# Four pairs of FFN gate blocks as two-by-two block products, seven in place of eight

## The chip, the cores and the metric

One core of a Trainium2 chip runs the whole program. The metric is the device time of one execution in microseconds; three runs of the kernel before gave 1250.42 to 1250.91, median 1250.7. Five engines work side by side, each on its own queue in order: TensorE (PE) multiplies, VectorE (DVE) and ScalarE (ACT) do elementwise work, GpSimd (POOL) does little here, and SyncE (SP) issues the loads.

## The reference

Two layers of a decoder trunk, all in float32, on 256 tokens of width 1024. Each layer is a norm, a wide input projection, three token mixers with gates, an output projection and then the feed-forward part. What the change touches is only this:

```
h = rmsnorm(x, norm_ffn[l])                     # 256 x 1024
x = x + (silu(h @ w_ffn_gate[l]) * (h @ w_ffn_up[l])) @ w_ffn_down[l]   # 1024 x 2816, 2816 x 1024
```

## The kernel before

Tokens lie as two tiles of 128 (t = 0, 1). A weight matrix is cut into blocks of 512 output columns, and the 1024 input features of a block into units of four rows of 128: a unit is one load of 1 MB (`load`, L982) into one of three raw buffers (`wr`). For accuracy each operand is split in a high part, rounded to the matmul's format ("hi", a cast on ScalarE, `conv_hi`, L1004), and the rest ("lo", a subtraction on VectorE of two SBUF inputs, `conv_lo`, L1010). A half unit (two rows of 128 by 512 columns, 1024 elements a partition) is converted at a time, into four rotating pairs of tiles (`wh`, `wl`). `products` (L1035) then issues, for each 128-row slice and each t, three matmuls of 512 columns: hi x hi, hi x lo, lo x hi (L1059 to L1061), so 24 per unit and 48 per block, into two PSUM banks of the pool `acc` (four banks). Four more banks (`sc`) serve the mixers and the transposes.

The order is written out by hand, in Python, at build time. The list `units` holds the units in order; in the FFN it is gate block 0 and up block 0 interleaved unit by unit, then gate b, up b for b = 1 to 4, then one block of the last 256 gate and 256 up columns, then the two down blocks. While a unit is multiplied there are four slots, one after every six matmuls; at each, `pump` runs the small steps that are due (`defer(n, ...)`: n slots later; `push`: a list of steps, one a slot), and one hi or one lo of a later unit is issued. `flush(key)` runs pumps until nothing with that key is left, so it puts all of it ahead of what comes next on every queue. At the start of unit i the load of unit i + 3 is issued.

A gate block is evicted by a tanh on ScalarE (L900) and a combine on VectorE (L904); an up block by a multiply on VectorE (L910), and its result is transposed on TensorE in two groups of four (`T_pair`, L297), each of which goes back to SBUF by a hi on ScalarE (L302) and a lo on VectorE (L309). Working tiles of 4 KB a partition come from the pool `s4` (19 tiles).

## Time and profile before

| | before |
|---|---|
| runs, median (lowest to highest) | 1250.7 us (1250.42 to 1250.91) |
| profiled execution, its own time | 1250.75 us |
| its span | 1248.9 us |
| busy TensorE / VectorE / ScalarE / GpSimd | 1238.5 / 786.4 / 659.6 / 34.8 us |
| mean granted TensorE clock | 0.999 |
| loads | 217 MB, 1 MB each, 5.0 us from issue to landing |

Busy time is the sum of the instructions' times on an engine; an instruction that waits inside for something the profile does not show counts as busy. The span runs from the first to the last instruction. All times of rows are microseconds from the span's start, means are in ns.

### The profile page before, as it was taken

Reading aid. Unit: us, or ns where it says so; the run is one execution under the profiler, and the core shown is the slowest. Engines: PE = TensorE matmul, PEld = TensorE weight load, DVE = VectorE, ACT = ScalarE, POOL = GpSimd, SP = SyncE. Lnnn points to the kernel's source line nnn. Section 1 sums busy time; section 2 is a strip of 40 time slices with the busy share of each in tenths; the row PEclk is TensorE's granted clock in tenths of the full one; section 3 lists DMA queues with packets and bytes.
Section 4 is the critical chain, followed back from the end, with each engine's and each line's share of the span. In section 5 each row is a group of like instructions: output and inputs, shape, how many; then the busy total and the mean of one; then the engine's idle time right before and its main releaser. Section 6 shows DMA issues by size and latency. Waiting matters only on the chain.

```text
span 1248.9 us, 17348 instructions
## 1 busy us (share of the span) xinstructions
PE 1238.5 (99%) x6894; PEld 1080.8 (87%) x6894; DVE 786.4 (63%) x1248; ACT 659.6 (53%) x999; POOL 34.8 (3%) x43
## 2 busy tenths in 40 slices
PE   9999999999999999999999999999999999999997
PEld 7999899999888888888889989898988888888886
DVE  5555567768566676565555565687775767656644
ACT  6433566766545455444454345667745445544442
POOL 1000000100000000000000000000000100000000
PEclk9999999999999999999999999999999999999999
DMA  8666445544655555555555543445456455555561
GB/s 280 213 207 196 154 167 169 163 144 168 201 169 169 170 189 181 186 184 185 185 184 187 189 156 129 148 157 169 136 203 199 138 168 182 189 188 182 178 219 59
DMA packets 114145, 219.82 MB, mean 176 GB/s; under 512 B 4168, under 2 KB 11336, under 8 KB 114064
## 3 DMA queue, kind: packets, MB, share of 16 engines
q1 hardware_dynamic: 113104, 217.07, 53.2%
q0 software_dynamic: 384, 0.84, 0.3%
q8 instruction: 54, 0.88, 0.3%
q10 hardware_dynamic: 576, 0.81, 0.2%
q14 instruction: 27, 0.22, 0.1%
HBM read 217.16 MB, written 1.54 MB: 175 GB/s over the span
## 4 chain that ended last, share of the span: by engine, by line
PE 98%; DMA 0%; issue 0%; DVE 0%; ACT 0%; POOLq 0%; POOL 0%; SPq 0%; DVEq 0%
PE acc L1060 22%; PE acc L1061 22%; PE acc L1059 22%; PE acc L1075 7%; PE acc L1074 7%; PE acc L1073 7%; PE tp L297 2%; PE sc L383 1%; PE sc L487 1%; PE sc L618 1%; PE sc L617 1%; PE sc L382 0%; PE sc L488 0%; PE tp L653 0%; PE acc L1025 0%; DMA x<-in_x_dram 0%
## 5 line engine op out<-in xcount | busy, mean ns | idle before, releaser
L1010 DVE TENSOR_TENSOR wl<-wr,wh 128x1024 fp32r<-128x1024 f32 x402 | 490.5, 1224 | 319.5 <-ACT wh L1004 317.0
L1004 ACT CAST wh<-wr 128x1024 fp32r<-128x1024 f32 x402 | 421.2, 1050 | 404.2 <-PE acc L1061 273.6
L1059 PE MATMUL acc<-wh,s 128*128 128x512 f32 x1220 | 488.8, 401 | 0.0
L1060 PE MATMUL acc<-wl,s 128*128 128x512 f32 x1220 | 476.0, 390 | 0.5 <-DVE wl L1108 0.5
L1061 PE MATMUL acc<-wh,s 128*128 128x512 f32 x1220 | 476.4, 390 | 0.0
L1061 PEld LDWEIGHTS acc<-wh,s 128*128 128x128 f32 x1220 | 229.3, 188 | 49.1
L1060 PEld LDWEIGHTS acc<-wl,s 128*128 128x128 f32 x1220 | 229.8, 188 | 45.0 <-DVE wl L1108 1.4
L1059 PEld LDWEIGHTS acc<-wh,s 128*128 128x128 f32 x1220 | 229.6, 188 | 44.2 <-issue 0.6
L1073 PE MATMUL acc<-s,wh 128*128 128x256 f32 x768 | 222.8, 290 | 0.0
L1075 PE MATMUL acc<-s,wl 128*128 128x256 f32 x768 | 217.4, 283 | 0.0
L1074 PE MATMUL acc<-s,wh 128*128 128x256 f32 x768 | 217.1, 283 | 0.0
L1074 PEld LDWEIGHTS acc<-s,wh 128*128 128x128 f32 x768 | 147.1, 192 | 0.3
L1073 PEld LDWEIGHTS acc<-s,wh 128*128 128x128 f32 x768 | 147.1, 191 | 0.3
L1075 PEld LDWEIGHTS acc<-s,wl 128*128 128x128 f32 x768 | 146.9, 191 | 0.0
L629 ACT ACTIVATE e<-e,sm 128x128 f32<-128x128 f32 x64 | 28.6, 448 | 9.8 <-DVE sm L622 9.6
L302 ACT CAST s<-tp 128x512 fp32r<-128x512 f32 x30 | 17.6, 587 | 27.2 <-PE tp L297 27.2
L305 ACT ACTIVATE s<-tp,gT 128x256 fp32r<-128x256 f32 x44 | 18.4, 472 | 18.7 <-PE tp L297 18.2
L297 PE MATMUL tp<-ident,s 128*128 128x128 f32 x184 | 27.5, 272 | 0.0
L297 PEld LDWEIGHTS tp<-ident,s 128*128 128x128 f32 x184 | 22.7, 140 | 5.2
L309 DVE TENSOR_TENSOR s<-tp,s 128x512 fp32r<-128x512 f32 x30 | 20.8, 692 | 10.1 <-ACT s L302 7.5
L312 DVE SCALAR_TENSOR_TENSOR s<-tp,gT,s 128x256 fp32r<-128x256 f32 x44 | 19.1, 478 | 12.4 <-ACT s L305 12.4
L622 DVE CUSTOM_DVE_ANT_0 e<-sc,bias_t 128x128 f32<-128x128 f32 x32 | 9.3, 289 | 24.6 <-PE sc L618 24.6
(173 smaller groups left out, 830.1 us busy)
## 6 DMA issues: line engine op xcount, KB each, us to landing
wr<-in_w_in_dram SPq DMA_DIRECT2D x107, 1024.0 KB, 5.1
wr<-in_w_ffn_gate_dram SPq DMA_DIRECT2D x20, 1024.0 KB, 5.0
wr<-in_w_ffn_up_dram SPq DMA_DIRECT2D x20, 1024.0 KB, 5.0
wr<-in_w_ffn_down_dram SPq DMA_DIRECT2D x20, 1024.0 KB, 5.1
wr<-in_w_branch_diff_dram SPq DMA_DIRECT2D x8, 1024.0 KB, 5.0
wr<-in_w_branch_ret_dram SPq DMA_DIRECT2D x8, 1024.0 KB, 5.0
wr<-in_w_out_dram SPq DMA_DIRECT2D x8, 1024.0 KB, 5.0
wr<-in_w_branch_dil_dram SPq DMA_DIRECT2D x4, 1024.0 KB, 5.1
```

Of the source, the lines that this page charges most:

```text
L297: T.transpose(pt[:, (2 * j + t) * P:(2 * j + t + 1) * P], srcs[t][:, j * P:(j + 1) * P], ident)
L309: V.tensor_tensor(lo[:, c0:c0 + 2, :], ptv, hi[:, c0:c0 + 2, :].bitcast(F32), op=ALU.subtract)
L312: V.scalar_tensor_tensor(lo[:, c0 + j, :], ptv[:, j, :], scale[j], hi[:, c0 + j, :].bitcast(F32), op0=ALU.mult, op1=ALU.subtract)
L629: A.activation(e[:, c], e[:, c], AF.Exp, bias=s_[:, 2 * m + qb:2 * m + qb + 1], scale=-1.0, accum_out=s_[:, 4 + 2 * m + qb:5 + 2 * m + qb])
L1004: A.copy(h, grans[i][0][:, ks, :])
L1010: V.tensor_tensor(l, grans[i][0][:, ks, :], pr[0].bitcast(F32), op=ALU.subtract)
L1059: T.matmul(o, sh, h[:, k, :], start=first, stop=False)
L1060: T.matmul(o, sh, l[:, k, :], start=False, stop=False)
L1061: T.matmul(o, sl, h[:, k, :], start=False, stop=last)
L1073: T.matmul(o, h[:, k, fs], xh[:, kk, :], start=first, stop=False)
L1074: T.matmul(o, h[:, k, fs], xl[:, kk, :], start=False, stop=False)
L1075: T.matmul(o, l[:, k, fs], xh[:, kk, :], start=False, stop=last)
```

## The change

Gate blocks 1 and 2 are taken as one block of 1024 columns, and so are 3 and 4, in both layers: four such pairs. For each 256 input features, the tokens form a two-by-two matrix of 128 x 128 blocks (token half by feature half) and the weights a two-by-two matrix of 128 x 512 blocks. In place of eight block products, seven products of sums are accumulated, each over four units, in seven PSUM banks (`Block7`, `products7`), each with the three matmuls of the split. A unit now holds 256 rows by 1024 columns, 1 MB as before.

The sums of weights are made on GpSimd (`sums7`: a subtraction of 1024 elements and two of 512 per unit) into two `s4` tiles; they are issued two units ahead. They are then converted like weights: seven blocks of 512 columns a unit, as parts of two, one, two and two blocks. The sums of tokens are made once per layer and feature group on GpSimd (`sums`), cast on ScalarE and subtracted on VectorE. After the last unit the seven accumulators are added up to the two gate blocks by seven additions on VectorE and a copy on ScalarE (`gate7`).

The conversions of all units go through one routine, `feed`, which issues the next hi or lo if fewer than four tile pairs are in use. The order of blocks is now: the pair of gates, then its two up blocks. The first unit of a pair flushes the evictions and the key "sums", the first up block behind it flushes "ffn". The second group of transposes of an up block is deferred by three slots more in place of two.

```diff
@@ -86,6 +86,22 @@
         self.accs = None
+class Block7:
+    nat = True
+    ORDER = ((1, 0, 0), (2, 0, 1), (3, 1, 0), (5, 2, 0), (7, 2, 1), (6, 3, 0), (4, 3, 1))
+    def __init__(self, w, npairs, tokens, steps, needs=None):
+        self.w, self.nks, self.tokens, self.steps = w, [2] * npairs, tokens, steps
+        self.needs = needs or {}
+        self.acc = {}
 @with_exitstack
 def trunk(ctx, tc, x_in, w_in, w_branch_ret, w_branch_diff, w_branch_dil, w_out, diff_lambda, rel_bias,
           w_ffn_gate, w_ffn_up, w_ffn_down, norm_final, gains, onehot, bmask, rot, decay, out):
@@ -890,7 +906,7 @@
         def ffn_h(z, w, dst):
             for c in range(w // S):
-                defer(2 + 2 * c, lambda c=c: T_pair([z[t][:, c * S:(c + 1) * S] for t in range(2)], dst, 2 * c, None),
+                defer(2 + 3 * c, lambda c=c: T_pair([z[t][:, c * S:(c + 1) * S] for t in range(2)], dst, 2 * c, None),
                       "ffn")
         def ffn_gate(zg, w):
@@ -910,13 +926,63 @@
                 V.scalar_tensor_tensor(z[t][:, :w], z[t][:, :w], st["nrm"].rsq[t], zu[t], op0=ALU.mult, op1=ALU.mult)
             ffn_h(z, w, dst)
+        L["z"] = []
         def ev_ffn_gate(accs):
-            L["z"] = ffn_gate(accs, 512)
+            L["z"].append(ffn_gate(accs, 512))
         def ev_ffn_up(accs):
             dst = new_T()
             L["hT"].append(dst)
-            ffn_up(L["z"], accs, 512, dst)
+            ffn_up(L["z"].pop(0), accs, 512, dst)
+        def sums(j):
+            nb, c = j // 2, 2 * (j % 2)
+            if c == 0:
+                L["sm", nb] = (S4([P, 2, 4, P], F32R), S4([P, 2, 4, P], F32R))
+            hi, lo = L["kf"][nb]
+            shi, slo = (t[:, j % 2] for t in L["sm", nb])
+            tmp = S4([P, 2, 512])
+            a = tmp[:, 0, :].rearrange("p (k t) -> p k t", t=S)
+            s_ = tmp[:, 1, :].rearrange("p (i t) -> p i t", t=P)
+            a11, a21, a12, a22 = a[:, 0, 0:P], a[:, 0, P:S], a[:, 1, 0:P], a[:, 1, P:S]
+            G.tensor_tensor(a, hi[:, c:c + 2, :].bitcast(F32), lo[:, c:c + 2, :].bitcast(F32), op=ALU.add)
+            G.tensor_tensor(s_[:, 0, :], a21, a22, op=ALU.add)
+            G.tensor_tensor(s_[:, 2, :], a11, a21, op=ALU.subtract)
+            G.tensor_tensor(s_[:, 1, :], s_[:, 0, :], a11, op=ALU.subtract)
+            G.tensor_tensor(s_[:, 3, :], a12, s_[:, 1, :], op=ALU.subtract)
+            defer(3, lambda: A.copy(shi, s_), "sums")
+            defer(4, lambda: V.tensor_tensor(slo, s_, shi.bitcast(F32), op=ALU.subtract), "sums")
+        def tokens7(j):
+            nb, c = j // 2, 2 * (j % 2)
+            out = {}
+            for pr, k, t in ((1, c, 0), (2, c + 1, 0), (4, c + 1, 1)):
+                out[pr] = tuple(a[:, k, t * P:(t + 1) * P] for a in L["kf"][nb])
+            for pr, i in ((5, 0), (6, 1), (7, 2), (3, 3)):
+                out[pr] = tuple(a[:, j % 2, i, :] for a in L["sm", nb])
+            return out
+        def gate7(acc):
+            u = S4([P, 2, 512])
+            c0, c1 = S4([P, 2, 512]), S4([P, 2, 512])
+            def add(o, a, b):
+                V.tensor_tensor(o, acc[b], a, op=ALU.add)
+            def rest():
+                add(u[:, 0, :], u[:, 0, :], 6)
+                add(u[:, 1, :], u[:, 0, :], 5)
+                add(u[:, 0, :], u[:, 0, :], 7)
+                add(c1[:, 0, :], u[:, 1, :], 3)
+                add(c1[:, 1, :], u[:, 0, :], 5)
+                add(c0[:, 1, :], u[:, 0, :], 4)
+                for n, c in enumerate((c0, c1)):
+                    defer(1 + 2 * n, lambda c=c: L["z"].append(ffn_gate([c[:, 0, :], c[:, 1, :]], 512)), "ffn")
+            return {3: lambda: A.copy(u[:, 0, :], acc[1]), 5: lambda: add(c0[:, 0, :], u[:, 0, :], 2), 4: rest}
    ...
@@ -960,12 +1026,14 @@
         paired(Block(cols(w_out[layer], 0), K8, lambda: L["mT"],
                      ev_x(0, lambda: Norm((1, layer))), True, {0: "mT0", 1: "mT1"}),
                Block(cols(w_out[layer], 512), K8, lambda: L["mT"], ev_x(1, None), True, {0: "mT0", 1: "mT1"}))
-        for b in range(5):
-            if b == 0:
-                paired(ffn_block(wg, 0, ev_ffn_gate, {0: set_kt("kf"), 1: "norm1"}), ffn_block(wu, 0, ev_ffn_up, {1: "fin"}))
-            else:
-                single(ffn_block(wg, b, ev_ffn_gate))
-                single(ffn_block(wu, b, ev_ffn_up))
+        def push_sums():
+            flush("fin")
+            push([lambda j=j: sums(j) for j in range(4)], "sums")
+        paired(ffn_block(wg, 0, ev_ffn_gate, {0: set_kt("kf"), 1: "norm1"}), ffn_block(wu, 0, ev_ffn_up, {1: push_sums}))
+        for b in (1, 3):
+            single(Block7(cols(wg, b * 512, 1024), 4, tokens7, gate7, {0: "sums"}))
+            single(ffn_block(wu, b, ev_ffn_up, {0: "ffn"}))
+            single(ffn_block(wu, b + 1, ev_ffn_up))
         single(Block(lambda k0, nk: [wg[k0 * P:(k0 + nk) * P, 2560:2816], wu[k0 * P:(k0 + nk) * P, 2560:2816]],
                      K8, lambda: L["kf"], ev_ffn_last, True))
         KD = [4] * 5 + [2]
@@ -984,6 +1052,12 @@
             return
         b, g = units[i]
         nk = b.nks[g]
+        if isinstance(b, Block7):
+            raw = wr_p.tile([P, 4, 512], F32, tag="wr", name=nm("wr"))
+            D.dma_start(raw.rearrange("p (k c) n -> p k (c n)", k=2),
+                        b.w(2 * g, 2)[0].rearrange("(k p) n -> p k n", p=P))
+            grans[i] = [raw]
+            return
         raw = wr_p.tile([P, nk, 512], F32, tag="wr", name=nm("wr"))
         c = 0
...
-    def halves(i):
-        nk = units[i][0].nks[units[i][1]] if i < len(units) else 0
-        return [(i, p, slice(p * 2, p * 2 + 2)) for p in range(nk // 2)]
-
-    def conv_hi(i, p, ks):
+    def sums7(i):
+        raw = grans[i][0]
+        t13, t24 = S4([P, 2, 512]), S4([P, 2, 512])
+        tts[i] = (t13, t24)
+        G.tensor_tensor(t13, raw[:, 1:4:2, :], raw[:, 0:2, :], op=ALU.subtract)
+        G.tensor_tensor(t24[:, 0, :], raw[:, 3, :], t13[:, 0, :], op=ALU.subtract)
+        G.tensor_tensor(t24[:, 1, :], raw[:, 2, :], t24[:, 0, :], op=ALU.subtract)
+    tts = {}
+    due = {"unit": 1, "part": 0, "lo": None, "live": 2}
+    def source(i, p):
+        if isinstance(units[i][0], Block7):
+            return (grans[i][0][:, 0:3:2, :], grans[i][0][:, 3:4, :], *(t for t in tts[i]))[p]
+        return grans[i][0][:, 2 * p:2 * p + 2, :]
+    def nparts(i):
+        return 4 if isinstance(units[i][0], Block7) else units[i][0].nks[units[i][1]] // 2
+    def feed(i):
+        if due["lo"] is not None:
+            l, raw, h = due["lo"]
+            V.tensor_tensor(l, raw, h.bitcast(F32), op=ALU.subtract)
+            due["lo"] = None
+            return True
+        u, p = due["unit"], due["part"]
+        if u >= len(units) or u > i + 2 or due["live"] >= 4:
+            return False
+        raw = source(u, p)
+        n = raw.shape[1]
         h = wh_p.tile([P, 2, 512], F32R, tag="wh", name=nm("wh"))
-        A.copy(h, grans[i][0][:, ks, :])
-        grans[i].append([h, None])
-
-    def conv_lo(i, p, ks):
         l = wl_p.tile([P, 2, 512], F32R, tag="wl", name=nm("wl"))
-        pr = grans[i][1 + p]
-        V.tensor_tensor(l, grans[i][0][:, ks, :], pr[0].bitcast(F32), op=ALU.subtract)
-        pr[1] = l
+        A.copy(h[:, 0:n, :], raw)
+        grans[u].append((h, l))
+        due["lo"] = (l[:, 0:n, :], raw, h[:, 0:n, :])
+        due["live"] += 1
+        due["unit"], due["part"] = (u, p + 1) if p + 1 < nparts(u) else (u + 1, 0)
+        return True
+    def ready(i, n):
+        while len(grans[i]) - 1 < n or (due["lo"] is not None and len(grans[i]) - 1 == n):
+            assert feed(i), (i, n, due)
...
@@ -1035,6 +1141,7 @@
     def products(i, slots, between=None):
         b, g = units[i]
         nk = b.nks[g]
+        ready(i, nparts(i))
         parts = grans[i][1:]
         xh, xl = b.kts()[g]
         first_g, last_g = g == 0, g == len(b.nks) - 1
@@ -1062,6 +1169,7 @@
                         if kk == 0 and t == 1 and between is not None:
                             between()
                         tick(6)
+                due["live"] -= 1
             else:
                 for fc in range(4):
                     fs = slice(fc * P, (fc + 1) * P)
@@ -1074,7 +1182,36 @@
                         T.matmul(o, h[:, k, fs], xl[:, kk, :], start=False, stop=False)
                         T.matmul(o, l[:, k, fs], xh[:, kk, :], start=False, stop=last)
                         tick(3)
+                due["live"] -= 1
         return last_g
+    def products7(i, slots):
+        b, g = units[i]
+        first, last = g == 0, g == len(b.nks) - 1
+        x7 = b.tokens(g)
+        if last:
+            steps = b.steps(b.acc)
+        work = 0
+        for n, (pr, part, half) in enumerate(b.ORDER):
+            if first:
+                b.acc[pr] = (ACC if pr in (1, 2, 6, 4) else SC)()
+            ready(i, part + 1)
+            h, l = grans[i][1 + part]
+            o, (sh, sl) = b.acc[pr], x7[pr]
+            T.matmul(o, sh, h[:, half, :], start=first, stop=False)
+            T.matmul(o, sh, l[:, half, :], start=False, stop=False)
+            T.matmul(o, sl, h[:, half, :], start=False, stop=last)
+            if n == 6 or b.ORDER[n + 1][1] != part:
+                due["live"] -= 1
+            if last and pr in steps:
+                steps[pr]()
+            work += 6
+            if work >= SLOT:
+                work -= SLOT
+                slots(0)
+            else:
+                feed(i)
+        feed(i)
     SLOT = 12
     cur[0] = "start"
@@ -1129,11 +1266,9 @@
                 need()
             else:
                 flush(need)
-        todo = [lambda f=f, hv=hv: f(*hv) for hv in halves(i + 1)[1:] + halves(i + 2)[:1] for f in (conv_hi, conv_lo)]
-
         if i == len(units) - 2:
-            while todo:
-                todo.pop(0)()
+            while feed(i):
+                pass
             flush("pre")
             flush("norm0")
             products_tail(i, b.evac)
@@ -1141,16 +1276,20 @@
         def slots(n):
             pump()
-            if todo:
-                todo.pop(0)()
+            feed(i)
+            if n == 0 and i + 2 not in tts and isinstance(units[i + 2][0], Block7):
+                sums7(i + 2)
         def second():
             first(1)
-            conv_hi(*halves(1)[0])
-            conv_lo(*halves(1)[0])
+            feed(0)
+            feed(0)
+        if isinstance(b, Block7):
+            products7(i, slots)
+            grans.pop(i)
+            continue
         last = products(i, slots, second if i == 0 else None)
         grans.pop(i)
-        while todo:
-            todo.pop(0)()
         if last:
             defer(1, lambda b=b: b.evac(b.accs), "evac")
```

## Rows read from the trace of the kernel before

**Rows 1.** Page, parts 1 and 4: busy us, share of the span, instructions; the chain's shares.

```profile
PE 1238.5 (99%) x6894; PEld 1080.8 (87%) x6894; DVE 786.4 (63%) x1248; ACT 659.6 (53%) x999; POOL 34.8 (3%) x43
...
PE 98%; DMA 0%; issue 0%; DVE 0%; ACT 0%; POOLq 0%; POOL 0%; SPq 0%; DVEq 0%
```

**Rows 2.** Timeline of PE in the FFN: start us, us, engine, line, operation.

```profile
478.29 0.39 PE L1059 MATMUL acc<-wh,s 128*128 128x512 f32 x1
...
481.01 0.39 PE L1059 MATMUL acc<-wh,s 128*128 128x512 f32 x1
...
489.18 0.60 PE L297 MATMUL tp<-ident,s 128*128 128x128 f32 x4
489.54 0.48 PE L1059 MATMUL acc<-wh,s 128*128 128x512 f32 x1
489.85 0.40 PE L1060 MATMUL acc<-wl,s 128*128 128x512 f32 x1
```

**Rows 3.** Timeline of DVE there; in brackets the idle time before, and what ended it.

```profile
480.94 1.23 DVE L1010 TENSOR_TENSOR wl<-wr,wh 128x1024 fp32r<-128x1024 f32 x1 [1.50 <-ACT wh L1004]
483.66 1.23 DVE L1010 TENSOR_TENSOR wl<-wr,wh 128x1024 fp32r<-128x1024 f32 x1 [1.50 <-ACT wh L1004]
484.80 1.40 DVE L910 SCALAR_TENSOR_TENSOR s<-s,rstd,acc 128x512 f32<-128x512 f32 x2
```

**Rows 4.** Groups of POOL, whole span: count, then busy us, mean ns, idle before.

```profile
masks.py:199 POOL TENSOR_SCALAR_AFFINE_SELECT ident<-ident 128x128 f32<-128x128 f32 x1 | 0.3, 294 | 0.1
masks.py:197 POOL MEMSET ident<- 128x128 f32 x1 | 0.2, 206 | 0.3 <-POOLq L1173 0.3
L159 POOL MEMSET nhalf<- 128x8 f32 x1 | 0.1, 106 | 0.0
```

**Rows 5.** Timelines of POOL, DVE and ACT where POOL and DVE meet.

```profile
274.69 1.01 POOL L689 TENSOR_TENSOR sm<-sm,nhalf 128x4 f32<-128x4 f32 x1 [40.80 <-DVE sm L688]
290.10 2.08 POOL L689 TENSOR_TENSOR sm<-sm,nhalf 128x4 f32<-128x4 f32 x1 [14.40 <-DVE sm L688]
995.26 0.70 POOL L812 TENSOR_TENSOR sm<-sm,nhalf 128x2 f32<-128x2 f32 x1 [15.06 <-DVE sm L810]
...
289.25 0.69 DVE L735 TENSOR_TENSOR s<-s,s 128x512 f32<-128x512 f32 x1
289.86 0.16 DVE L688 TENSOR_SCALAR sm<-sm 128x4 f32<-128x4 f32 x1
290.09 1.23 DVE L1010 TENSOR_TENSOR wl<-wr,wh 128x1024 fp32r<-128x1024 f32 x1
...
994.91 0.27 DVE L810 TENSOR_SCALAR sm<-sm 128x1 f32<-128x1 f32 x2
995.49 1.23 DVE L1010 TENSOR_TENSOR wl<-wr,wh 128x1024 fp32r<-128x1024 f32 x1 [0.31 <-issue]
...
993.88 1.05 ACT L1004 CAST wh<-wr 128x1024 fp32r<-128x1024 f32 x1
```

**Rows 6.** Groups of DVE and ACT, 473.7 to 519.2 us.

```profile
L910 DVE SCALAR_TENSOR_TENSOR s<-s,rstd,acc 128x512 f32<-128x512 f32 x4 | 2.8, 742 | 0.0
L309 DVE TENSOR_TENSOR s<-tp,s 128x512 fp32r<-128x512 f32 x4 | 2.8, 692 | 0.4
...
L1004 ACT CAST wh<-wr 128x1024 fp32r<-128x1024 f32 x16 | 16.8, 1052 | 18.7 <-PE acc L1061 18.7
L302 ACT CAST s<-tp 128x512 fp32r<-128x512 f32 x4 | 2.3, 587 | 3.0 <-PE tp L297 3.0
```

**Rows 7.** Timelines of SP and DVE; page, part 6: us to landing.

```profile
442.84 6.77 SPq L994 DMA_DIRECT2D wr<-in_w_ffn_gate_dram  x2
...
462.06 1.40 DVE L910 SCALAR_TENSOR_TENSOR s<-s,rstd,acc 128x512 f32<-128x512 f32 x2
...
wr<-in_w_ffn_gate_dram SPq DMA_DIRECT2D x20, 1024.0 KB, 5.0
```

**Rows 8.** Windows: us, busy of PE, PEld, DVE, ACT, POOL, clock, DMA share, GB/s.

```profile
1240.00:1249.00 9.00, 1.50 (x13) 1.29 (x11) 3.41 (x11) 2.38 (x6) 0.56 (x1) 0.81 0.31 117
```

## The prediction

> **What bounds the kernel now.** Read first the busy shares and the chain of waits: TensorE is busy 99% of the span and the chain runs through it for 98% [rows 1]; VectorE stands at 63%, ScalarE at 53%, GpSimd at 3%. So a matmul less is time less, as long as the others keep up; an average can't say whether they do, so the FFN stage is read by itself. Next the TensorE timeline of that stage: 12 matmuls of 512 columns take 2.72 us, 0.2267 us each, and four transposes add 0.36 and 0.08 of slower matmul behind them, about 0.45 [rows 2]. A unit of 24 matmuls is 5.44 us. Then VectorE there [rows 3]: one low-part subtraction ("lo") of 1024 elements takes 1.23 us, 1.14 to 1.15 from start to start, two per unit, and it idles 1.50 us before one while it waits for ScalarE's cast ("hi"), which waits for TensorE to free a tile. So VectorE has room in this stage, but only four converted tiles of lead.
>
> The profiled execution took 1250.75 us, 1.85 more than its span of 1248.9; the median of the runs is 1250.7, so the sum is made on 1250.75.
>
> **What is removed.** A pair of gate blocks costs 96 matmuls, the seven products 4 x 21 = 84. 12 x 0.2267 = 2.72 us a pair; two pairs a layer, 5.44; four in all, 10.88. Without any new wait the result is 1250.75 - 10.88 = 1239.9.
>
> **What is added to GpSimd.** Per gate unit one subtraction of 1024 elements and two of 512 (2048 elements, three instructions), 16 times; per layer four token sums, each one of 512 and four of 128 (1024 elements, five instructions). The trace has no long two-input operation on GpSimd. Nearest rows [rows 4]: a memset of 8 elements 106 ns, of 128 elements 206 ns, so 0.10 us fixed and 0.83 ns an element for a write alone; the select, one read more, 294 ns, so 0.69 ns for a read. Low end: 0.83 ns an element. High end: each input costs a whole one-input operation, 2 x 1.48 = 2.97 ns. I take a write and two reads, 0.83 + 2 x 0.69 = 2.2 ns, since that counts each access once. A unit's sums are then 2.35 + 2 x 1.23 = 4.8 us (2.0 to 6.4), a token sum 1.23 + 4 x 0.38 = 2.75 us (1.35 to 3.5). The Trainium skill (GPSIMD Engine Reference, section 3.1) measures 4497 ns for 2048 elements; by it the unit's sums are about 4.6 us as an estimate and the forecast some 3 us lower.
>
> **What is added to VectorE and ScalarE.** A gate unit of 4.76 us (21 matmuls) has three and a half tiles to convert, not two: VectorE 3 x 1.15 + 0.61 = 4.06 us (0.61 is the start-to-start of 512 elements from SBUF [rows 5]), ScalarE 3 x 1.05 + 0.59 = 3.7 us [rows 6]. Both fit, VectorE barely. The seven output sums (about 0.69 each, as the eviction of rows 6) and the four combines stand behind the lo's of the next unit and a half in the queue: six sums, one lo and four combines are 4.2 + 1.2 + 2.8 = 8.2 us, and TensorE has three parts of 2.72 us converted by then. Cost nothing; if VectorE arrives late, they add to its lateness. The seven accumulators leave one bank for transposes, so the second pair waits for the first one's eviction: hidden while VectorE is on time. The same bytes are loaded, issued some 14 us ahead; a load now waits for the sums that read its buffer too, and that is late only where the sums are already the wait. Moving the conversions of all other units to one feed keeps their order of one hi or lo a slot: nothing.
>
> **The first new wait, token sums.** GpSimd's order before the first gate block of a layer is: sums of gate unit 0, token sum 0, sums of gate unit 1, token sums 1 to 3. The flush on "sums" puts all four casts of token sums on ScalarE ahead of the cast of part 3 of gate unit 0, so that part waits for all six. Weights are issued at 442.84, and with 5.0 us to landing the first sums start at 447.8; the second issue of that row, at about 449.2, the end of 442.84 + 6.77 less the issue itself, lands at 454.2, in time. GpSimd alone: 452.6, 455.4, 460.2, then 468.4. Cast 0.59, hi 1.05, lo 1.23: ready at 471.3. TensorE ends the up block at 461.9, the flush makes it wait for that block's eviction (two of 0.74, started only now, as its transposes are ahead of the first product) 1.4 us, transposes 0.45, and five products 3.4: it asks at 467.2. So 4.1 + 1.4 = 5.5 us a layer [rows 6, 7], as much as the matmuls save, even if GpSimd and VectorE don't touch each other.
>
> **The second, GpSimd against VectorE.** They do [rows 5]. GpSimd's small power operation takes 1.01 us at 274.69; the one at 290.10, 10 ns behind a lo of 1.23 us, takes 2.08: it waited the lo out. The other way: the lo at 995.49 has its cast since 994.93 and VectorE free since 995.18, and starts 0.31 us late for nothing that the profile names, 0.23 after a GpSimd operation began. So an operation with two SBUF inputs on VectorE and one that reads on GpSimd exclude each other. Those rows show it for two to four elements read by GpSimd; I take it that one that reads throughout holds throughout.
>
> The Trainium skill (SBUF — State Buffer, Who interferes with whom) says just that: the shared read port is held "for the whole instruction", by whichever came first, and two SBUF inputs on VectorE count. The row of 2.08 us agrees for a waiting GpSimd; for a long GpSimd operation no row shows it. By the rule the sum is the one below; if only the rows' 0.2 to 0.3 us per operation counted, it would be close to the rival without exclusion.
>
> Sum by exclusion, per layer, from the landing of the first gate weights to the moment when part 3 of the fourth gate unit is due: 14.0 (447.8 to 461.9) + transposes 0.9 + 4 x 4.76 - 1.36 = 32.6 us.
> First block: GpSimd 4 x 4.8 + 4 x 2.75 = 30.2; VectorE 14 full lo's (two of the up unit, twelve gate) 16.1, four halves 2.4, four token lo's 2.4: 20.9. Together 51.1, over by 18.5.
> Second block: 19.2 + 18.5 = 37.7, over by 5.1.
> 23.6 - 5.44 = 18.2 a layer, 36.3 in two layers. Neither queue is without gaps: in each block a cast of 1.05 and one of 0.6 stand once between the two engines, 1.7 x 4 = 7, an estimate from these casts. Forecast 1250.75 + 36.3 + 7 = **1294 us**. At GpSimd's low end the blocks are over by 1.7 and nothing, 1243; at its high end by 28.0 and 11.4, which gives 1250.75 + 68 + 7 = 1326.
> In waits of several us TensorE's clock could fall: its mean is 0.81 in the closing stretch, where TensorE is busy 1.50 of 9 us [rows 8]. At 1.2 in place of 2.4 GHz a matmul takes 0.2267 us more, so twelve of them after each long stall 2.7 us a layer; since the stage is then set by the other two engines I count nothing and leave it to the range.
>
> **Rivals.**
> 1. No exclusion for long operations, GpSimd at 2.2 ns: the first wait alone, 5.5 - 5.44 a layer, 1251 us (1249 to 1258 with small VectorE delays). For it: both delays are seen at operations that read two to four elements, and the one of VectorE was only 0.31 us. Against it: the 2.08 us, a full lo waited out [rows 5].
> 2. Faster: GpSimd's sums stay hidden. Place: token sum 3 of the first block. Without exclusion its wait is gone when the six sums (8192 elements, 26 instructions) take 16.5 in place of 20.6 us, at (16.5 - 2.6) / 8192 = 1.7 ns an element; only the 1.4 us of eviction is left and the time is 1250.75 - 2 x (5.44 - 1.4) = 1243. With exclusion the change gains below about 1.0 ns: the first block then holds 12288 elements and 3.2 us of fixed cost beside the 20.9, and is over by 2 us, which with its 1.7 of gaps is less than 5.44. So 1240 to 1247. For it: the low end; against it: the two reads, and the rows of exclusion.
> 3. GpSimd slower than taken, 2.5 to 3 ns: 1315 to 1326 and more if the clock falls.
> That the matmuls fall away is no rival: the loop over seven products fixes their count.
>
> **Chances.** Forecast, 1265 to 1315: 0.62. Rival 1: 0.15. Rival 2: 0.13. Rival 3: 0.10. The range leaves out rival 2, most of rival 3 and a little of rival 1: 1250 to 1318. Faster by over 0.2% (2.5 us, about what a measurement of this kernel can tell from no change) 0.14, within it 0.07 (the middle of rival 1), slower 0.79.
>
> **What will show it.** GpSimd busy about 2 x 49 = 98 us more or longer, since blocked time counts as busy; a unit's 1024-element subtraction at 2.4 us alone. Lo's that start late with GpSimd named or nothing shown before them. TensorE idle some 19 to 20 us in the first gate block of each layer, most of it before product 6 of gate unit 0, and 5 to 8 in the second. 48 matmuls fewer. Wrong if GpSimd's row is under 1.7 ns an element, if lo's start while a long GpSimd operation runs, or if TensorE has no gap at the first gate unit.

## The result, and the profile after

The changed kernel takes 1295.07 us (median of four runs, 1294.75 to 1295.63) against 1250.7 before (four runs as well): a ratio of 1.0355, 95% interval 1.0337 to 1.0373. The forecast was 1294. The profiled execution has a span of 1292.8 us.

The changed kernel's page, parts 1 and 4 (busy us, share of the span, instructions; then the shares of the chain that ended last), answering [rows 1]:

```profile
PE 1242.2 (96%) x6846; PEld 1076.4 (83%) x6846; DVE 883.5 (68%) x1316; ACT 688.7 (53%) x1043; POOL 175.4 (14%) x131
...
PE 88%; DVE 5%; POOL 4%; issue 1%; ACT 0%; DMA 0%; POOLq 0%; SPq 0%; DVEq 0%; ACTq 0%
```

TensorE has 48 matmuls fewer, and its chain is broken: VectorE and GpSimd now hold 9% of it. TensorE's busy time went up although it does less; matmuls at half clock, shown below, are part of that.

Where the time went is read from the evictions of the up blocks (L910 before, L926 after), which mark the ends of the stages. In the first layer those of up blocks 0, 2 and 4 start at 462.06, 507.53 and 552.98 before and at 465.12, 525.47 and 575.22 after. So the stretch that ends with the first pair's second up block is 17.9 us late, the next one 4.3 more, 22.2 a layer and 44.5 in two, counting the second layer as the first (its own markers end 44.6 late). With the 2.72 us of matmuls saved in each, the first block lost 20.7 us and the second 7.0. The markers of blocks 2 and 4 (the first two lines before, the last two after):

```profile
507.53 1.40 DVE L910 SCALAR_TENSOR_TENSOR s<-s,rstd,acc 128x512 f32<-128x512 f32 x2
552.98 1.40 DVE L910 SCALAR_TENSOR_TENSOR s<-s,rstd,acc 128x512 f32<-128x512 f32 x2
...
525.47 1.39 DVE L926 SCALAR_TENSOR_TENSOR s<-s,rstd,acc 128x512 f32<-128x512 f32 x2
575.22 1.40 DVE L926 SCALAR_TENSOR_TENSOR s<-s,rstd,acc 128x512 f32<-128x512 f32 x2
```

Two windows of the changed kernel, the first and the second gate block of that layer with some of the up units (columns as in [rows 8]):

```profile
461.50:500.00 38.50, 22.93 (x85) 16.71 (x84) 29.88 (x22) 15.84 (x20) 27.39 (x24) 0.87 0.25 82
516.00:560.00 44.00, 39.27 (x170) 30.93 (x169) 42.93 (x37) 23.85 (x29) 27.02 (x12) 0.96 0.49 163
```

TensorE stands idle for 15.6 and 4.7 us, and its mean clock is below 1. In the second window VectorE is busy 42.93 of 44: it looks like the bound, but much of that time is waiting inside instructions, as the next rows show.

GpSimd's groups in the changed kernel (count, busy us, mean ns, idle before), answering [rows 4]:

```profile
L1077 POOL TENSOR_TENSOR s<-wr 128x1024 f32<-128x1024 f32 x16 | 48.0, 3000 | 48.6 <-DMA wr<-in_w_ffn_gate_dram 48.6
L1079 POOL TENSOR_TENSOR s<-wr,s 128x512 f32<-128x512 f32 x16 | 32.7, 2042 | 1.3
L1078 POOL TENSOR_TENSOR s<-wr,s 128x512 f32<-128x512 f32 x16 | 31.5, 1966 | 1.3
L950 POOL TENSOR_TENSOR s<-s,s 128x512 f32<-128x512 f32 x8 | 12.2, 1526 | 0.0
```

The means hold waits. Single instructions, from the timelines of the same two engines inside the first gate block (first VectorE, then GpSimd), answering [rows 5]:

```profile
481.34 2.31 DVE L1097 TENSOR_TENSOR wl<-wr,wh 128x1024 fp32r<-128x1024 f32 x1
483.57 2.88 DVE L1097 TENSOR_TENSOR wl<-wr,wh 128x512 fp32r<-128x512 f32 x1
486.38 2.30 DVE L1097 TENSOR_TENSOR wl<-s,wh 128x1024 fp32r<-128x1024 f32 x1
...
476.31 2.35 POOL L1077 TENSOR_TENSOR s<-wr 128x1024 f32<-128x1024 f32 x1
...
480.42 2.15 POOL L1079 TENSOR_TENSOR s<-wr,s 128x512 f32<-128x512 f32 x1
482.53 3.37 POOL L1077 TENSOR_TENSOR s<-wr 128x1024 f32<-128x1024 f32 x1
485.98 1.62 POOL L1078 TENSOR_TENSOR s<-wr,s 128x512 f32<-128x512 f32 x1
```

They take turns. The lo that begins at 481.34 ends at 483.65, 1.08 us after GpSimd's operation before it ended (482.57). GpSimd's next one is stamped 482.53, but takes 3.37 us where 2.35 is its own time: it ends 2.25 us after that lo. The next lo, of 512 elements and 0.68 us alone, takes 2.88 and ends 0.55 us after GpSimd (485.90). GpSimd's next, of 512 elements and 1.62 us, ends 1.15 us after that lo (487.60 and 486.45): it was held too, and such an operation alone takes 1.26 to 1.30 us, as this one of run e8 below, which began while VectorE ran nothing with two SBUF inputs:

```profile
520.47 1.30 POOL L1020 TENSOR_TENSOR s<-wr,s 128x512 f32<-128x512 f32 x1
```

The wait of each lies inside its own busy time, so neither "idle before" nor the waits name it: it is read from a duration against the same shape elsewhere.

Instructions of TensorE in that block that had waited (in brackets how long, and for what), changed kernel; the last two lines follow the first wait without one:

```profile
465.91 0.34 PE L313 MATMUL tp<-ident,s 128*128 128x128 f32 x1 [4.00 <-DVE s L926]
466.57 0.90 PE L313 MATMUL tp<-ident,s 128*128 128x128 f32 x3 [0.31 <-DVE s L926]
479.86 0.79 PE L1201 MATMUL sc<-wh,s 128*128 128x512 f32 x1 [8.20 <-DVE s L325]
486.51 0.50 PE L1202 MATMUL sc<-wl,s 128*128 128x512 f32 x1 [1.15 <-DVE wl L1097]
488.74 0.50 PE L1202 MATMUL sc<-wl,s 128*128 128x512 f32 x1 [1.26 <-DVE wl L1097]
490.97 0.50 PE L1202 MATMUL acc<-wl,s 128*128 128x512 f32 x1 [0.58 <-DVE wl L1097]
...
468.55 0.63 PE L1201 MATMUL acc<-wh,s 128*128 128x512 f32 x1
468.97 0.63 PE L1202 MATMUL acc<-wl,s 128*128 128x512 f32 x1
```

The long one is product 7 of the first gate unit, the fifth in the order of issue. Behind the 4.00 us matmuls follow each other at 0.42 us, not 0.23: from 467 to 469 us the granted clock is 0.50.

What product 7 waits for, on VectorE: the lo's of token sums 1 to 3 (L956), then the eviction of the first transposes (L325):

```profile
470.14 1.11 DVE L956 TENSOR_TENSOR s<-s,s 128x512 fp32r<-128x512 f32 x1 [3.62 <-ACT s L955]
473.60 1.08 DVE L956 TENSOR_TENSOR s<-s,s 128x512 fp32r<-128x512 f32 x1 [2.35 <-ACT s L955]
477.04 2.17 DVE L956 TENSOR_TENSOR s<-s,s 128x512 fp32r<-128x512 f32 x1 [2.35 <-ACT s L955]
479.13 0.68 DVE L325 TENSOR_TENSOR s<-tp,s 128x512 fp32r<-128x512 f32 x1
```

VectorE is idle for 8.3 us here until ScalarE casts the token sums, and ScalarE waits for GpSimd, which works without a break from 447.62 to 476.36. So in this stretch it is GpSimd's results that are late.

### The profile page after: what moved, and what is told of

It is laid out like the page before. It is cut to its first block, busy times and chain, and to the rows that moved or that the text cites. A ratio compares the mean times of both kernels' runs of the same rounds, so it can differ in the third digit from the quotient of the medians.

```text
span 1292.8 us, 17519 instructions
## 1 busy us (share of the span) xinstructions
PE 1242.2 (96%) x6846; PEld 1076.4 (83%) x6846; DVE 883.5 (68%) x1316; ACT 688.7 (53%) x1043; POOL 175.4 (14%) x131
## 4 chain that ended last, share of the span: by engine, by line
PE 88%; DVE 5%; POOL 4%; issue 1%; ACT 0%; DMA 0%; POOLq 0%; SPq 0%; DVEq 0%; ACTq 0%
PE acc L1166 18%; PE acc L1167 18%; PE acc L1168 18%; PE acc L1183 7%; PE acc L1182 7%; PE acc L1181 7%; DVE wl L1097 4%; PE tp L313 2%; POOL s L950 1%; POOL s L1077 1%; PE sc L399 1%; PE sc L503 1%; POOL s L1078 1%; POOL s L1079 1%; PE sc L634 1%
## 5 line engine op out<-in xcount | busy, mean ns | idle before, releaser
L1097 DVE TENSOR_TENSOR wl<-wr,wh 128x1024 fp32r<-128x1024 f32 (+1 forms) x402 | 505.7, 1268 | 245.7 <-ACT wh L1107 243.3
L1107 ACT CAST wh<-wr 128x1024 fp32r<-128x1024 f32 (+1 forms) x402 | 412.1, 1033 | 345.3 <-PE acc L1168 205.3
L1166 PE MATMUL acc<-wh,s 128*128 128x512 f32 x1092 | 438.0, 401 | 0.0
L1168 PE MATMUL acc<-wh,s 128*128 128x512 f32 x1092 | 426.4, 390 | 0.0
L1167 PE MATMUL acc<-wl,s 128*128 128x512 f32 x1092 | 425.9, 390 | 0.5 <-DVE wl L1245 0.5
L1168 PEld LDWEIGHTS acc<-wh,s 128*128 128x128 f32 x1092 | 205.1, 188 | 44.0
L1167 PEld LDWEIGHTS acc<-wl,s 128*128 128x128 f32 x1092 | 205.6, 188 | 40.3 <-DVE wl L1245 1.4
L1166 PEld LDWEIGHTS acc<-wh,s 128*128 128x128 f32 x1092 | 205.5, 188 | 39.4 <-issue 0.6
L1097 DVE TENSOR_TENSOR wl<-s,wh 128x1024 fp32r<-128x1024 f32 x32 | 54.7, 1735 | 4.1 <-ACT wh L1107 3.6
L1077 POOL TENSOR_TENSOR s<-wr 128x1024 f32<-128x1024 f32 x16 | 48.0, 3000 | 48.6 <-DMA wr<-in_w_ffn_gate_dram 48.6
L1107 ACT CAST wh<-s 128x1024 fp32r<-128x1024 f32 x32 | 33.7, 1052 | 25.5 <-PE sc L1203 10.7
L705 POOL TENSOR_TENSOR sm<-sm,nhalf 128x4 f32<-128x4 f32 x8 | 10.3, 1282 | 251.8 <-DVE sm L704 251.8
```

The source lines that it names most:

```text
L1077: G.tensor_tensor(t13, raw[:, 1:4:2, :], raw[:, 0:2, :], op=ALU.subtract)
L1097: V.tensor_tensor(l, raw, h.bitcast(F32), op=ALU.subtract)
L1107: A.copy(h[:, 0:n, :], raw)
L1166: T.matmul(o, sh, h[:, k, :], start=first, stop=False)
L1167: T.matmul(o, sh, l[:, k, :], start=False, stop=False)
L1168: T.matmul(o, sl, h[:, k, :], start=False, stop=last)
```

## The experiments

All ran with three rounds against the kernel before, which gave 1250.4 to 1250.7 in each group. Theory A is the forecast's: a GpSimd operation that reads SBUF and a VectorE operation with two SBUF inputs exclude each other. B: GpSimd's results are only late. C: the form with seven products costs by itself. O: the order of the token sums costs. D is formed on the way: the one PSUM bank for transposes. Runs e2, e8 and e9 have ten times each, the others four.

| run | us | ratio, 95% interval |
|---|---|---|
| the change | 1295.07 | 1.0355, 1.0337 to 1.0373 |
| e1, no token sums | 1273.09 | 1.0178, 1.0161 to 1.0195 |
| e2, no weight sums | 1247.93 | 0.9979, 0.9969 to 0.9988 |
| e3, no sums | 1241.93 | 0.9930, 0.9915 to 0.9945 |
| e4, weight sums unused | 1268.55 | 1.0140, 1.0125 to 1.0155 |
| e5, written, not read | 1241.62 | 0.9929, 0.9914 to 0.9944 |
| e6, token sums earlier | 1298.18 | 1.0384, 1.0369 to 1.0400 |
| e7, token sums on VectorE | 1285.39 | 1.0278, 1.0262 to 1.0293 |
| e8, before plus unused sums | 1250.54 | 0.9998, 0.9988 to 1.0007 |
| e9, one weight sum | 1254.52 | 1.0025, 1.0016 to 1.0035 |
| e10, two weight sums | 1258.14 | 1.0060, 1.0043 to 1.0077 |
| e11, e9 with later transposes | 1245.46 | 0.9959, 0.9944 to 0.9974 |
| e12, the change with later transposes | 1295.50 | 1.0360, 1.0342 to 1.0377 |

**e1, without the sums of tokens.**

```diff
-            push([lambda j=j: sums(j) for j in range(4)], "sums")
-                out[pr] = tuple(a[:, j % 2, i, :] for a in L["sm", nb])
+                out[pr] = tuple(a[:, c + i % 2, i // 2 * P:(i // 2 + 1) * P] for a in L["kf"][nb])
```

> Left out: the sums of tokens (products 3, 5, 6, 7 take plain token blocks). Theory A, GpSimd's reading operations and VectorE's operations with two SBUF inputs exclude each other: both blocks of a layer now cost what the second one did, 7.0 us of TensorE waits in the changed kernel, so 1250.7 + 2 x (2 x 7.0 - 5.44) = 1268 us, 1262 to 1272. Theory B, GpSimd's results are only late and VectorE is not slowed by it: no wait is left, 1240 to 1244. Theory C, the seven-product form costs by itself (conversions, one transpose bank, flushes): little changes, 1285 to 1295.

1273.1: above A's 1268 by 5 and outside its range by 1, far from B and C. The first block, marked as above, is 9.2 us late in gross and not 7.0, the second 7.3.

**e2, without the sums of weights.**

```diff
-        t13, t24 = S4([P, 2, 512]), S4([P, 2, 512])
-        tts[i] = (t13, t24)
-        G.tensor_tensor(t13, raw[:, 1:4:2, :], raw[:, 0:2, :], op=ALU.subtract)
...
+        tts[i] = (raw[:, 0:2, :], raw[:, 2:4, :])
```

> Left out: the sums of weights (parts 2 and 3 are converted from the plain weights); the sums of tokens stay on GpSimd. A: GpSimd has 11 us per layer to do, all of it possible before the first gate unit; only the flushed eviction of the first up block is left, 1242 to 1248. B: the same, so this run does not part A from B. C: 1275 to 1290.

1247.9, at the edge of the range: the token sums alone leave a small gain. The cost of the token sums is 22 us where the weight sums stand beside them (the change against e1) and 6 where they don't (e2 against e3), so it isn't a wait of their own. What they share can be the exclusion or GpSimd's queue, in which they stand behind weight sums, so this run doesn't part A from B. No run makes the token sums without using them, so how much of the 22 us is exclusion and how much is late results is not shown.

**e3, without both.** The two edits above together.

> Left out: both kinds of sums; the seven products, conversions, output additions, flushes and banks stay. A and B: the 48 matmuls are gained nearly whole, 1240 to 1243. C: 1265 or more.

1241.9: C falls. The seven products, the work of 56 whole tile conversions in place of 32, the output sums and the flushes gain 8.8 of the 10.9 us. In the first layer's stretch from 440 to 560 us TensorE is busy 119.26 of 120 us (before, 120.00), so 0.74 of the missing 1.04 a layer is idle time. It lies in two waits for the one bank of the transposes, of which this is the first (e3):

```profile
470.75 0.63 PE L313 MATMUL tp<-ident,s 128*128 128x128 f32 x4 [0.37 <-DVE s L325]
```

**e4, weight sums made and not used** (no token sums).

```diff
-            return (grans[i][0][:, 0:3:2, :], grans[i][0][:, 3:4, :], *(t for t in tts[i]))[p]
+            return (grans[i][0][:, 0:3:2, :], grans[i][0][:, 3:4, :], grans[i][0][:, 0:2, :], grans[i][0][:, 2:4, :])[p]
```

> Left out: the sums of tokens; the sums of weights are made on GpSimd as in the change, but nobody reads them (parts 2 and 3 come from the plain weights). A: VectorE is blocked as before, so near the kernel without token sums, 1258 to 1268. B: nobody waits for GpSimd, so as without any sums, 1240 to 1243.

1268.6, 0.55 us beyond the upper end of A's range, 27 above e3: B falls as an account of the weight sums. Nobody converts GpSimd's results, and 27 of the 31 us by which e1 is above e3 are there: it is what GpSimd does to VectorE. Loads, which also wait for the sums that read their buffer, are not it: in the first layer's FFN of e4 (440 to 600 us) no conversion and no matmul waits for one. The lo's of 1024 elements in 510 to 560 us take 1526 ns on average, and in e3 1220:

```profile
L1096 DVE TENSOR_TENSOR wl<-wr,wh 128x1024 fp32r<-128x1024 f32 x21 | 31.4, 1526 | 1.2 <-ACT wh L1106 1.2
```

```profile
L1092 DVE TENSOR_TENSOR wl<-wr,wh 128x1024 fp32r<-128x1024 f32 x23 | 27.7, 1220 | 6.2 <-ACT wh L1102 6.0
```

(The first fence is e4's group of lo's in that stretch, the second e3's.)

**e5, GpSimd writes as long, and reads nothing** (no token sums).

```diff
-        G.tensor_tensor(t13, raw[:, 1:4:2, :], raw[:, 0:2, :], op=ALU.subtract)
...
+        for t in (t13, t24[:, 0, :], t24[:, 1, :]):
+            for _ in range(3):
+                G.memset(t, 0.01)
```

> Left out: the sums of tokens; each of the three weight sums of a unit is three memsets of its output tile (a constant in place of the sum), so GpSimd is busy about 2.9 + 1.6 + 1.6 us a unit, as long as the sums alone, and TensorE's parts still wait for it, but it reads nothing. Theory A, a GpSimd operation that reads SBUF and a VectorE operation with two SBUF inputs exclude each other: no lo is delayed, 1241 to 1246. Theory A', any GpSimd operation excludes it: as the kernel without token sums, 1265 to 1275.

1241.6, as without any sums, although GpSimd is busy 47.5 us in 440 to 560 us. It's the reading that costs, not a busy GpSimd. The dependence is tested less: the memsets wait for no load and run through from 448.1 to 497.7 us, so the tiles of the second block are ready before their use. In the first block casts waited for GpSimd for 3.7 us in all, at no cost. The lo's beside the memsets (e5, 461.5 to 500 us, where GpSimd is busy 34.1 of 38.5) are untouched:

```profile
L1096 DVE TENSOR_TENSOR wl<-wr,wh 128x1024 fp32r<-128x1024 f32 x12 | 14.3, 1219 | 0.2
L1096 DVE TENSOR_TENSOR wl<-s,wh 128x1024 fp32r<-128x1024 f32 x8 | 9.8, 1225 | 4.0 <-ACT wh L1106 3.9
```

**e6, token sums one unit earlier.**

```diff
-        paired(ffn_block(wg, 0, ev_ffn_gate, {0: set_kt("kf"), 1: "norm1"}), ffn_block(wu, 0, ev_ffn_up, {1: push_sums}))
+        paired(ffn_block(wg, 0, ev_ffn_gate, {0: set_kt("kf"), 1: push_sums}), ffn_block(wu, 0, ev_ffn_up))
```

with `flush("norm1")` ahead of `flush("fin")` in `push_sums`.

> Same result as the change; the token sums are pushed one unit earlier, so token sum 0 is ahead of the first weight sums, all four ahead of the second, and their casts lie in the slots of the up unit. A: the same work in the same window, at most the start is 1 us earlier: 1288 to 1295. Theory O, the first block's cost is the order (the flush puts the four casts in front of everything): the first block falls to the second's 7 us, 1266 to 1275.

1298.2: O falls; A's range (to 1295) is missed by 3 us on the slow side. The waits of TensorE in the first block are 3.6, 3.3 and 2.7 us and smaller ones where the change had 4.0 and 8.2, and behind them more matmuls follow at 0.42 us. That this makes up the 3 us is argued, not shown.

**e7, token sums on VectorE.**

```diff
-            G.tensor_tensor(a, hi[:, c:c + 2, :].bitcast(F32), lo[:, c:c + 2, :].bitcast(F32), op=ALU.add)
-            G.tensor_tensor(s_[:, 0, :], a21, a22, op=ALU.add)
...
+            V.tensor_tensor(a, hi[:, c:c + 2, :].bitcast(F32), lo[:, c:c + 2, :].bitcast(F32), op=ALU.add)
+            V.tensor_tensor(s_[:, 0, :], a21, a22, op=ALU.add)
...
```

> Same result as the change; the token sums are made on VectorE. A: per layer 11 us of GpSimd become about 4 x (0.61 + 4 x 0.22) = 6 us of VectorE in the same window, 5 us less: 1285, 1280 to 1290. O: the chain through GpSimd loses 11 us, the first block falls to the second's: 1266 to 1275.

1285.4, as A's sum has it: taking work off GpSimd and giving it to the engine that seems full is a gain of 9.7 us. By A the two share one budget and VectorE does the work in less of it (0.68 us for 512 elements and 0.29 for 128, against GpSimd's 1.28 and 0.45); that no token sum is late behind weight sums any more can be part of the gain.

**e8, the kernel before, with unused sums.**

```diff
...
+                units[-1][0].extra = True
...
+    def extra(i):
+        raw = grans[i][0]
+        t13, t24 = S4([P, 2, 512]), S4([P, 2, 512])
+        G.tensor_tensor(t13, raw[:, 1:4:2, :], raw[:, 0:2, :], op=ALU.subtract)
+        G.tensor_tensor(t24[:, 0, :], raw[:, 3, :], t13[:, 0, :], op=ALU.subtract)
+        G.tensor_tensor(t24[:, 1, :], raw[:, 2, :], t24[:, 0, :], op=ALU.subtract)
...
+            if n == 0 and units[i + 2][0].extra:
+                extra(i + 2)
```

`extra` is set for gate blocks 1 to 4.

> The kernel before, with the same 16 weight sums on GpSimd for the units of gate blocks 1 to 4 and nobody reading them. A: two gate blocks and two up blocks take 45.5 us and hold 16 lo's, 18.4 us, and 22 us of GpSimd alone: 40.4 us fit, so the lo's get longer (mean in that stretch 1.6 us or more) and the time moves little, 1250.5 to 1256. A theory by which GpSimd's work itself costs TensorE time (a transfer, a port of TensorE): 1260 or more.

1250.5: nothing. The same operations delay the lo's here too (510 to 560 us, first e8, then the kernel before):

```profile
L1012 DVE TENSOR_TENSOR wl<-wr,wh 128x1024 fp32r<-128x1024 f32 x18 | 26.0, 1446 | 13.5 <-ACT wh L1006 13.5
...
L1010 DVE TENSOR_TENSOR wl<-wr,wh 128x1024 fp32r<-128x1024 f32 x18 | 22.1, 1225 | 18.0 <-ACT wh L1004 18.0
```

1446 ns against 1225 before, but VectorE still waits 13.5 us for casts: two tiles a unit leave room. (1600 ns was expected for a stretch that GpSimd fills; here it works 13.7 of the 50 us.) So the delay costs only where the conversions have no slack.

**e9 and e10, fewer weight sums** (no token sums): one of three, two of three; memsets stand for the rest.

```diff
-        G.tensor_tensor(t24[:, 0, :], raw[:, 3, :], t13[:, 0, :], op=ALU.subtract)
-        G.tensor_tensor(t24[:, 1, :], raw[:, 2, :], t24[:, 0, :], op=ALU.subtract)
+        for _ in range(3):
+            G.memset(t24, 0.01)
```

This is e9; e10 leaves out only the second of the two lines, and its memsets write `t24[:, 1, :]`.

> Left out: the sums of tokens, and of a unit's weight sums the two of 512 elements (memsets stand for them); the one of 1024 elements stays. The ledger of theory A as a threshold: reading GpSimd 4 x 2.35 = 9.4 us and VectorE 18.5 in a block, 27.9 of 32.6 us: it fits, so nothing is lost but the flushed eviction: 1241.5 to 1245. If the loss goes in proportion to GpSimd's reading (43% of the 31 us by which the kernel without token sums is above the one without any): 1255.

> Left out: the sums of tokens, and the last of a unit's three weight sums (memsets stand for it). Ledger: 4 x (2.35 + 1.3) = 14.6 and 18.5, 33.1 of 32.6 us: over by 0.5, with the 1.7 of gaps 2.2 a block, so 1241.9 + 4 x 2.2 = 1251, 1243 to 1254. In proportion (67% of 31 us): 1263.

1254.5 and 1258.1. The ledger as a threshold misses: e9 is 12.6 us above e3 where its sum fits by 4.7 us a block, e10 is 4 us beyond its range. Most of what e9 lost stands in its second block (5.6 of 6.7 us in the first layer, by the markers), in one wait of TensorE (e9's timeline, then its windows from there):

```profile
517.98 1.09 PE L313 MATMUL tp<-ident,s 128*128 128x128 f32 x4 [2.74 <-DVE s L325]
```

```profile
515.00:518.00 3.00, 0.26 (x3) 0.05 (x1) 3.00 (x3) 0.49 (x1) 2.94 (x3) 0.87 0.78 298
518.00:521.00 3.00, 3.00 (x9) 2.52 (x10) 1.57 (x2) 1.16 (x2) 1.00 (x2) 0.50 0.18 14
521.00:524.00 3.00, 3.00 (x9) 2.32 (x8) 1.23 (x1) 1.48 (x2) 0.00 (x0) 0.50 0.90 326
524.00:527.00 3.00, 3.00 (x15) 2.48 (x14) 2.83 (x3) 1.62 (x4) 0.00 (x0) 1.00 0.03 10
```

The second group of transposes waits for the only free bank, which the first group's eviction on VectorE gives back, and that stands behind two lo's that GpSimd delays. After the wait the granted clock is 0.50, which is 1.2 GHz, for some 6 us: 9 instructions in 3 us and not 15. That is 2.7 us and 13 times 0.2 us, 5.3 in this layer: theory D. In the second layer the same wait of 2.74 us is followed by 8 slow matmuls. The ten times of e9 fall in two groups, three at 1251.6 to 1252.2 with a mean clock of 0.998 and seven at 1254.1 to 1255.2 with 0.995 or 0.996; the profile is of the longest. e10 has such a wait in its first block, which is part of why it is beyond its range:

```profile
473.98 1.04 PE L313 MATMUL tp<-ident,s 128*128 128x128 f32 x4 [2.94 <-DVE s L325]
```

**e11 and e12, the second transposes later**, in e9 and in the change.

```diff
-                defer(2 + 3 * c, lambda c=c: T_pair([z[t][:, c * S:(c + 1) * S] for t in range(2)], dst, 2 * c, None),
+                defer(2 + 6 * c, lambda c=c: T_pair([z[t][:, c * S:(c + 1) * S] for t in range(2)], dst, 2 * c, None),
```

> The kernel with one weight sum a unit (token sums and the two sums of 512 elements left out), and the second group of an up block's transposes deferred by six slots in place of three. Theory D: what that kernel lost, 1254.5 against 1241.9, is one TensorE wait of 2.74 us in the second block at those transposes, for the single PSUM bank that the seven accumulators leave, and the clock at half for 13 matmuls behind it (0.2 us each, 2.6 us). With the transposes later: 1254.5 - 2 x 5.3 = 1244, 1242 to 1247. If the loss is the longer lo's alone: 1252 to 1255.

> The change with the second transposes deferred by six slots. A: GpSimd's and VectorE's common work sets the length of both blocks, and the waits at the bank (8.2 us before product 7 in the first block, 2.2 in the second) only move to a later conversion: 1288 to 1296. D for the full change too: they go, 1270 to 1278.

1245.5: D holds for e9, 9.1 us come back. What is left, 3.5 us over e3, is half a microsecond more than the ledger's range for e9 allows. 1295.5: for the change itself the bank is not the limit. Its waits in the first block (e12's timeline) have only moved:

```profile
467.05 0.47 PE L313 MATMUL tp<-ident,s 128*128 128x128 f32 x1 [4.11 <-DVE s L926]
...
479.65 0.79 PE L1201 MATMUL acc<-wh,s 128*128 128x512 f32 x1 [5.97 <-ACT wh L1107]
482.64 0.80 PE L1202 MATMUL acc<-wl,s 128*128 128x512 f32 x1 [2.20 <-DVE wl L1097]
487.64 0.50 PE L1202 MATMUL sc<-wl,s 128*128 128x512 f32 x1 [0.62 <-DVE wl L1097]
489.87 0.50 PE L1202 MATMUL sc<-wl,s 128*128 128x512 f32 x1 [1.26 <-DVE wl L1097]
```

No version that makes and uses all the sums beats the kernel before. Whether one could is open. An estimate from the measured durations: spread evenly over the eight units of a pair, GpSimd needs 4 x (2.35 + 2 x 1.28) = 19.6 us and the lo's 20 x 1.15 + 4 x 0.61 = 25.4, 45.1 together, and TensorE 4 x 4.76 + 4 x 5.44 + 1.8 = 42.6. That is over by 2.5 where the saving is 2.7, and in turns each operation takes a little less than alone. So it is near a draw, and two other orders (e6, e12) have been tried.

## Why the prediction was right, step by step

- **The matmuls.** 10.9 us forecast, 8.8 measured (e3). 0.74 of the missing 1.04 us a layer is TensorE waiting for the one bank of the transposes, which the forecast had as hidden; the flushed eviction, forecast at 1.4, costs nothing there.
- **GpSimd's price.** A write and two reads, from three small rows, gave 2.35 us for 1024 elements and 1.23 for 512; alone they take 2.35 (476.31) and 1.26 to 1.30. The 128-element ones take 0.45, not 0.38. So a unit is 4.9 us (4.8 forecast) and a token sum 3.1 (2.75). This term carried the sum, and of all it rested on the thinnest rows; that it came out so near is in part luck. In rival 2 the first block at 1.0 ns an element is over by 3.8 us, not 2; nothing else changes by it.
- **The first wait.** There, but its place was wrong, and the idle time was forecast too long: 19 to 20 us in the first block, most of it before product 6, at the conversion of part 3. Measured are 15.6, of which 4.3 are the flush and 8.2 stand before product 7, one product earlier, whose bank is the one of the first transposes; their eviction stands behind the token lo's. The wait itself is GpSimd's results being late: its six sums take 28.7 us, where their own durations make 22.2 and the forecast had 20.6. The rest, some 6 us, is VectorE holding GpSimd up, an estimate from the same rows. The flushed eviction costs 4.3 us, not 1.4, since it stands behind a held lo of weights and token lo 0 too. The place doesn't matter for the time: with the token sums (e6) or the second transposes (e12) moved, the block is as long as it was or longer.
- **The exclusion.** Shown for the sums of weights: e4 (the cost without the dependence), e5 (a busy GpSimd without reading: no cost), e8 (the delay without the cost, where there is room). The Trainium skill (SBUF — State Buffer, Who interferes with whom) has whoever comes first hold the shared port for the whole instruction, for which no row of before spoke. The trace agrees: a lo of 0.68 us was held for 2.33 behind one GpSimd operation. The rival without exclusion (1251) is out by e4 and by these rows.
- **The ledger.** 18.5 + 1.7 and 5.1 + 1.7 us over forecast, 20.7 and 7.0 measured. With GpSimd's measured durations the sum would be 20.3 + 1.7 and 5.5 + 1.7. As a sum it held in the change and in e7 to a microsecond or two; e1's first block, 5.1 + 1.7 by the same sum, it missed by 2.4. That is closer than its terms are known: in turns an operation takes less than counted (1.08 us for the lo's 1.15, 2.25 for GpSimd's 2.35), and the 1.7 of gaps was never measured by itself. So the forecast's nearness, 1 us in 44, is in part luck; the mechanism is not. As a threshold it failed (e9): where the sum fits, single long waits still reach TensorE through anything that has a lead shorter than a GpSimd operation, there the bank of the transposes.
- **What was put at nothing.** The one bank: right for the change (e12), 0.4 us a block in e3, wrong for e9, 9 us with the clock (e11). The clock: matmuls at 0.42 us stand behind the long waits of the change (12 in the first block, 2.4 us); the other engines set the pace there, and e12 has them in other places at the same time. How much of the 7 us taken for gaps is in truth clock is open.
- **The marker.** "Wrong if lo's start while a long GpSimd operation runs" was badly put. By their stamps they do start; they don't end. GpSimd's busy time grew by 141 us, not 98: alone its sums would make about 103, the rest is time in which they were held, which the forecast had said would count.

## What to carry to other kernels

Here GpSimd was not a free engine beside VectorE: add its reading operations to VectorE's operations with two SBUF inputs, as one queue, and compare the sum with the stage. If it doesn't fit, reordering may not help (two tries here, e6 and e12, didn't), and giving the work to VectorE outright can be the smaller loss (e7). If it fits, look for what has less lead than one GpSimd operation lasts. In these profiles such a wait has no name: compare an instruction's duration with the same shape elsewhere.

## What the runs showed of the hardware that was not expected

An operation with one SBUF input was held as well. The changed kernel's timeline around GpSimd's first weight sum (VectorE, then GpSimd):

```profile
448.54 2.37 DVE L364 TENSOR_SCALAR rstd<-rstd 128x2 f32<-128x2 f32 x1
...
447.62 3.26 POOL L1077 TENSOR_TENSOR s<-wr 128x1024 f32<-128x1024 f32 x1
```

Two elements take 2.37 us and end with GpSimd's operation (450.91 and 450.88). In e6 the same one takes 1.26 us behind a shorter operation, and the two end within 0.03 us again (450.19, 450.16). Why one input was enough here no run shows.

In e9 a wait of 2.74 us was followed by some 6 us at a granted clock of 0.50. In the second layer of e10 a wait of 2.96 us at the same place (to 1093.68) was not: the clock is 1.00 from 1092 to 1098 us. In these runs the length of one such wait doesn't tell whether the clock falls.
